# A 2x2 block scheme with seven products for the feed-forward of a hybrid trunk layer

## The chip, the cores and the metric

The kernel runs on one core of a Trainium2 chip. The core has a matrix engine (TensorE, PE in the rows), a vector engine (VectorE, DVE), a scalar engine (ScalarE, ACT), GpSimd (POOL) and SyncE (SP), which here only issues DMA transfers. The metric is the device time of one execution in microseconds (us), the median of several runs.

## The reference

One layer over 1024 tokens of width 1024, in fp32. Three token mixers run on a combined projection of `h` and are concatenated; the rest is an output projection, a residual norm, a gated feed-forward of width 2816 (22 blocks of 128) with a gated per-layer embedding, and a second residual norm:

```
h = layer_norm(x, ln_in_g, ln_in_b)
...
mix = jnp.concatenate([o_a, o_b, o_c], axis=-1) @ w_out[i]
h = layer_norm(DEEPNORM_ALPHA * h + mix, ln1_g[i], ln1_b[i])
gate, up = jnp.split(h @ w_gate_up[i], 2, axis=-1)
ffn = (jax.nn.silu(gate) * up) @ w_down[i]
ple = jax.nn.sigmoid(h @ ple_w_gate[i]) * (p[i] @ ple_w_proj[i])
h = layer_norm(DEEPNORM_ALPHA * h + ffn + ple, ln2_g[i], ln2_b[i])
```

## The kernel before

Every product is made in three matmuls. An operand is split into a high part (a cast to the rounded format on ScalarE) and a low part (the subtraction `sub_lo`, L106, on VectorE, for one weight page in four on GpSimd); high by high, high by low and low by high are added in PSUM. A weight page is 128 x 1024; `wpage` loads and splits it.

The program text is straight-line; a framework schedules it and sets the order of each engine's queue. Each engine, and SP's DMA queue, works its instructions off in that order. Ahead of the change lie the input norm, projections, the three mixers and attention (to about 514.5 us); they stay as they are. Attention stores its output tiles `ta` to DRAM (`mix_d`, L755), 64 rows for each block.

Then follow four stages. The output projection runs twice over the eight token tiles, for either half of the columns (L767 to L789): it loads the mixers' outputs (`mixT`, L772), splits them, and takes 24 matmuls of 512 columns (`op`). In the second pass each tile is normed (`ln_stats`, `ln_apply`) and transposed into `hThi`/`hTlo`. The gate of the embedding (`pgt`, L793 to L805) goes through four quarters of 256 columns. The feed-forward goes through PARTS of three or four blocks f (L808 to L848): gate and up of a block, silu and product (`sil`, `act`), then for all eight tiles the down matmuls of the part (`dn`), added to `r_t` by VectorE (L844). In the last part each tile is normed and stored (`out`, L848).

## Time and profile before

| what | value |
|---|---|
| runs, us | 1439.05, 1440.24, 1440.18; median 1440.18 |
| profiled execution, span | 1436.9 us, 3.3 below the median |
| TensorE busy | 1393.6 us, 97% of the span |
| VectorE busy | 660.0 us, 46% |
| ScalarE busy | 420.3 us, 29% |
| GpSimd busy | 209.2 us, 15% |
| bytes moved by DMA | 133.69 MB, mean 93 GB/s |

Times in rows are from the start of the profiled span. What lies around the span (the 3.3 us) is taken as unchanged. Matmuls overlap in the trace, so the cost of one is the distance between starts, not its own duration.

### The profile page before, as it was taken

How to read it: one execution, taken by the hardware profiler on the slowest of the kernel's cores; microseconds unless marked ns; L12 is line 12 of the kernel's file. 1: busy time of each engine (PE TensorE's matmuls, PEld its weight loads, DVE VectorE, ACT ScalarE, POOL GpSimd, SP SyncE). 2: the span in 40 equal slices, each digit the busy share in tenths (PEclk: the TensorE clock that was granted, in tenths of full speed). 3: DMA queues.
4: the chain of work that ended last, by engine and by line, in shares of the span. 5: the costliest groups of instructions: out<-in, count | busy, mean ns of one | idle time of the engine just before them, and what ended most of it. 6: DMA issues, size and time to landing. Idle time of an engine off the chain costs nothing.

```text
span 1436.9 us, 18294 instructions
## 1 busy us (share of the span) xinstructions
PE 1393.6 (97%) x7264; PEld 1188.4 (83%) x7264; DVE 660.0 (46%) x1019; ACT 420.3 (29%) x791; POOL 209.2 (15%) x225
## 2 busy tenths in 40 slices
PE   6999999999899999999999999999999999999996
PEld 4888998987688878899988888888888888888885
DVE  7832695455778854973322232312332223223248
ACT  5542122452677733431221020120210211202100
POOL 3220111312233301520000000000000000000013
PEclk9999999999899999999999999999999999999999
DMA  8731021445944246232211110210311201202112
GB/s 325 263 101 59 28 67 45 146 169 183 337 111 104 60 137 225 74 122 77 86 44 44 45 59 30 73 45 15 88 44 35 69 30 44 74 16 73 30 44 103
DMA packets 55717, 133.69 MB, mean 93 GB/s; under 512 B 6736, under 2 KB 22096, under 8 KB 54096
## 3 DMA queue, kind: packets, MB, share of 16 engines
q1 hardware_dynamic: 55632, 132.52, 29.1%
q8 instruction: 57, 0.93, 0.3%
q14 instruction: 28, 0.23, 0.0%
HBM read 100.12 MB, written 32.37 MB: 92 GB/s over the span
## 4 chain that ended last, share of the span: by engine, by line
PE 67%; DVE 2%; ACT 2%; issue 1%; POOL 1%; DMA 1%; POOLq 0%; ACTq 0%; SPq 0%; DVEq 0%
PE gate L357 6%; PE dn L843 6%; PE gate L356 6%; PE gate L359 6%; PE up L359 6%; PE up L356 6%; PE up L357 6%; PE dn L840 6%; PE dn L839 6%; PE pgt L240 2%; PE pgt L241 2%; PE pgt L242 2%; PE pt L735 2%; PE op L783 1%; PE sc L715 1%
## 5 line engine op out<-in xcount | busy, mean ns | idle before, releaser
L117 ACT CAST whi<-raw 128x1024 fp32r<-128x1024 f32 (+3 forms) x101 | 104.7, 1037 | 607.0 <-PE dn L840 219.6
L106 DVE TENSOR_TENSOR wlo<-raw,whi 128x1024 fp32r<-128x1024 f32 (+3 forms) x77 | 99.5, 1294 | 177.4 <-ACT whi L117 136.0
L106 POOL TENSOR_TENSOR wlo<-raw,whi 128x1024 fp32r<-128x1024 f32 (+1 forms) x24 | 57.3, 2386 | 784.9 <-ACT whi L117 784.9
L844 DVE TENSOR_TENSOR r<-r,dn 128x1024 f32<-128x1024 f32 x56 | 68.0, 1220 | 161.7 <-PE dn L843 161.3
L357 PE MATMUL gate<-hTlo,whi 128*128 128x512 f32 x352 | 137.0, 389 | 0.0
L356 PE MATMUL gate<-hThi,whi 128*128 128x512 f32 x352 | 136.9, 389 | 0.0
L356 PE MATMUL up<-hThi,whi 128*128 128x512 f32 x352 | 136.9, 389 | 0.0
L357 PE MATMUL up<-hTlo,whi 128*128 128x512 f32 x352 | 136.9, 389 | 0.0
L840 PE MATMUL dn<-wlo,act 128*128 128x512 f32 x352 | 136.9, 389 | 0.0
L839 PE MATMUL dn<-whi,act 128*128 128x512 f32 x352 | 136.8, 389 | 0.0
L822 DVE TENSOR_TENSOR sil<-up,sil 128x512 f32<-128x512 f32 x44 | 28.3, 685 | 199.3 <-PE up L359 199.3
L359 PE MATMUL up<-hThi,wlo 128*128 128x512 f32 x352 | 108.7, 389 | 0.0
L359 PE MATMUL gate<-hThi,wlo 128*128 128x512 f32 x352 | 108.4, 389 | 0.0
L843 PE MATMUL dn<-whi,act 128*128 128x512 f32 x352 | 107.7, 389 | 0.0
L840 PEld LDWEIGHTS dn<-wlo,act 128*128 128x128 f32 x352 | 66.1, 188 | 13.8
L357 PEld LDWEIGHTS up<-hTlo,whi 128*128 128x128 f32 x352 | 66.1, 188 | 13.7
L359 PEld LDWEIGHTS up<-hThi,wlo 128*128 128x128 f32 x352 | 66.0, 188 | 13.7
L356 PEld LDWEIGHTS up<-hThi,whi 128*128 128x128 f32 x352 | 66.1, 188 | 13.7
L839 PEld LDWEIGHTS dn<-whi,act 128*128 128x128 f32 x352 | 66.1, 188 | 13.7
L357 PEld LDWEIGHTS gate<-hTlo,whi 128*128 128x128 f32 x352 | 66.1, 188 | 13.7
L843 PEld LDWEIGHTS dn<-whi,act 128*128 128x128 f32 x352 | 66.1, 188 | 13.7
L356 PEld LDWEIGHTS gate<-hThi,whi 128*128 128x128 f32 x352 | 66.1, 188 | 13.7
(275 smaller groups left out, 2982.3 us busy)
## 6 DMA issues: line engine op xcount, KB each, us to landing
raw<-in_w_gu_dram SPq DMA_DIRECT2D x44, 512.0 KB, 3.5
raw<-in_w_dn_dram SPq DMA_DIRECT2D x22, 512.0 KB, 3.9
mixT<-mix_d SPq DMA_DIRECT2D x16, 512.0 KB, 3.5
x<-in_x_dram SPq DMA_DIRECT2D x8, 512.0 KB, 6.6
h_d<-x SPq DMA_DIRECT2D x8, 512.0 KB, 5.0
pl_d<-plo SPq DMA_DIRECT2D x16, 256.0 KB, 4.6
hx<-h_d SPq DMA_DIRECT2D x16, 256.0 KB, 3.4
raw<-in_w_out_dram SPq DMA_DIRECT2D x8, 512.0 KB, 7.6
```

The source lines that it names most:

```text
L106: eng.tensor_tensor(out=lo, in0=src, in1=hi, op=ALU.subtract)
L117: nc.scalar.copy(out=hi[:, :w], in_=raw[:, :w])
L240: mm(ps, th, wh, start=(k == 0), stop=False)
L241: mm(ps, th, wl, start=False, stop=False)
L242: mm(ps, tl, wh, start=False, stop=(k == NK - 1))
L356: mm(pss[hf], wh, hThi[hf][:, k, :], start=(k == 0), stop=False)
L357: mm(pss[hf], wh, hTlo[hf][:, k, :], start=False, stop=False)
L359: mm(pss[hf], wl, hThi[hf][:, k, :], start=False, stop=(k == NK - 1))
L839: mm(ps[:, c], ah, wd[k][0][:, c], start=(k == 0), stop=False)
L840: mm(ps[:, c], ah, wd[k][1][:, c], start=False, stop=False)
L843: mm(ps[:, c], al, wd[k][0][:, c], start=False, stop=(k == nf - 1))
L844: V.tensor_tensor(out=r_t[t], in0=r_t[t], in1=ps, op=ALU.add)
```

## The change

*Pools.* The pools of the stages up to attention close before the output projection; later stages have pools of their own on the same bytes, whose tiles wait only for users of earlier tiles on these bytes.

*Output projection.* One pass over the eight tiles, both halves of the columns in turn, so `mixT` is loaded and split once. All eight pages of `w_out` are held. The normed rows `h1` and the transposed `hT` are also stored to DRAM.

*Gate of the embedding.* Two halves of 512 columns instead of four quarters; the sum of residual and embedding goes to DRAM (`r_d`).

*Gate and up.* For each block f the product of weights (gate and up rows by two halves of the 1024 inputs) and `hT` (two halves of inputs by two halves of tokens) is made of 7 products instead of 8, each of 4 x 3 matmuls of 512 columns. The sums of weight blocks (`block_sums`, 4 for each f) and of the blocks of `hT` are made on GpSimd; seven operand pairs for each f are split by ScalarE and VectorE. The result `x` goes to DRAM (`x_d`), and for each pair of blocks, j, `down_operands` makes four sums on GpSimd, splits them and stores them (`a_d`).

*Down.* Eleven pairs j in CHUNKS of one or two; in a chunk each tile pair (i, i+4) has 7 products with the operands reloaded (`a_load`, `x_load`, the latter split again). Of the twelve products of a chunk that ScalarE copies out of PSUM, GpSimd adds the copy to `r_t`; the other sixteen VectorE adds from PSUM. The last chunk norms and stores each row in halves.

```diff
-PARTS = ((0, 3), (3, 6), (6, 9), (9, 12), (12, 15), (15, 18), (18, 22))
...
-        mp = ctx.enter_context(tc.tile_pool(name="mp", bufs=1))
-        pp = ctx.enter_context(tc.tile_pool(name="pp", bufs=1, space=bass.MemoryType.PSUM))
+        wpool = ctx.enter_context(tc.tile_pool(name="wpool", bufs=1))
+        front = ExitStack()
+        mp = front.enter_context(tc.tile_pool(name="mp", bufs=1, reuse_waits="tile"))
+        pp = front.enter_context(tc.tile_pool(name="pp", bufs=1, space=bass.MemoryType.PSUM, reuse_waits="tile"))
...
+        def split(hi, lo, src):
+            nc.scalar.copy(out=hi, in_=src)
+            sub_lo(V, lo, src, hi)
...
+        def mix_load(t):
+            mx = op.tile([P, 2, NK, P], F32R, tag="mix", name=nm("mixT"), bufs=3)
+            mr = mx[:, 1].bitcast(F32)
+            dma(out=mr, in_=mix_d[t // 4][t % 4])
+            nc.scalar.copy(out=mx[:, 0], in_=mr)
+            sub_lo(V, mx[:, 1], mr, mx[:, 0])
+            return mx
...
+        wo = []
+        waiting = None
+        for t in range(NT):
+            hx = op.tile([P, D], F32, tag="hx", name=nm("hx"), bufs=2)
+            mx = mix_load(t)
+            dma(out=hx, in_=h_d[t])
+            if t == 0:
...
+            h1 = op.tile([P, D], F32, tag="h1", name=nm("h1"), bufs=2)
+            for hf in range(2):
+                cs = slice(hf * 512, hf * 512 + 512)
+                if t == 0:
+                    for u in range(4):
+                        wo.append(wpage(A["w_out"][hf * 4 + u]) if hf == 0 else
+                                  wpage(A["w_out"][hf * 4 + u], spot=(None if u == 0 else op)))
+                ps = ps_("Z", "op")
                 for k in range(NK):
...
-                V.scalar_tensor_tensor(out=r_t[t][:, cs], in0=hx, scalar=ALPHA, in1=ps, op0=ALU.mult, op1=ALU.add)
...
+                V.scalar_tensor_tensor(out=h1[:, cs], in0=hx[:, cs], scalar=ALPHA, in1=ps, op0=ALU.mult, op1=ALU.add)
+                if hf == 0 and waiting is not None:
+                    h_transposed(*waiting)
+            mv = ln_stats(h1, D, "l")
+            ln_apply(h1, h1, mv, ln1[:, 0, :], ln1[:, 1, :], G if t < 6 else V)
+            waiting = (t, h1)
+        h_transposed(*waiting)
+        op_ctx.close()
...
+        for hf in range(2):
+            wq = [wpage(A["w_pg"][hf * 4 + u]) for u in range(4)]
+            cs = slice(hf * 512, hf * 512 + 512)
+            for t in ((0, 1, 2, 3, 4, 5, 6, 7), (4, 5, 6, 7, 0, 1, 2, 3))[hf]:
+                pl = t2("cp", 3, "pl")
                 dma(out=pl, in_=pl_d[t][:, cs])
...
+                dma(out=hx, in_=h1_d[t][:, cs])
+                ps = ps_("Z", "pgt")
+                c = slice((t % 4) * P, (t % 4 + 1) * P)
+                for k in range(NK):
...
-            for f in range(f0, f1):
-                wg = wpage(A["w_gu"][f])
-                pgu = psu("gate")
-                T_mm([pgu[:, 0:512], pgu[:, 512:1024]], wg)
-                wu = wpage(A["w_gu"][NF + f])
-                pup = [psb("up"), psb("up")]
-                T_mm(pup, wu)
...
+        HOP = {1: HB[0, 0], 2: HB[1, 0], 3: HB[1, 1], 4: TB[4], 5: TB[1], 6: TB[2], 7: TB[3]}
...
+        def wpair(src, pool=None, tag="W", bufs=10):
+            w = (pool or wpool).tile([P, 2, 512], F32R, tag=tag, name=nm("wp"), bufs=bufs)
+            split(w[:, 0, :], w[:, 1, :], src)
+            return w
...
+            if sign > 0:
+                G.tensor_tensor(out=s1, in0=a21, in1=a22, op=ALU.add)
+                G.tensor_tensor(out=s2, in0=s1, in1=a11, op=ALU.subtract)
+                G.tensor_tensor(out=s3, in0=a11, in1=a21, op=ALU.subtract)
+                G.tensor_tensor(out=s4, in0=a12, in1=s2, op=ALU.subtract)
+                return {1: a11, 2: a12, 7: s3, 6: s2, 4: a22, 5: s1, 3: s4}
...
+        ORDER = (1, 2, 7, 6, 4, 5, 3)
+        BANK = {1: "Y", 6: "Y", 5: "Y", 3: "Y", 2: "Z", 7: "W", 4: "W"}
+        OPENS = (1, 2, 7)
...
+                g, u = pages
+                ops = block_sums(g[:, :512], g[:, 512:], u[:, :512], u[:, 512:], 1, s2k)
+                self.w = {m: wpair(ops[m]) for m in ORDER}
...
+            def product(self, m):
...
+                w, b = self.w[m], HOP[m]
+                for k in range(4):
...
+                    mm(o, w[:, 0, ks], b.at(0, k), start=(m in OPENS and k == 0), stop=False, skip_group_check=True)
+                    mm(o, w[:, 0, ks], b.at(1, k), start=False, stop=False, skip_group_check=True)
+                    mm(o, w[:, 1, ks], b.at(0, k), start=False, stop=(k == 3), skip_group_check=True)
+                x = self.x
+                if m in (1, 7, 6):
+                    c = t2("cp", 3)
+                    nc.scalar.copy(out=c, in_=o)
+                    setattr(self, f"c{m}", c)
+                elif m == 2:
+                    self.g0 = t2("g", 2)
+                    V.tensor_tensor(out=self.g0, in0=o, in1=self.c1, op=ALU.add)
+                    act(out=self.g0, in_=self.g0, func=AF.Silu)
+                elif m == 4:
+                    V.tensor_tensor(out=x[:, :512], in0=o, in1=self.c6, op=ALU.add)
+                    V.tensor_tensor(out=x[:, :512], in0=x[:, :512], in1=self.g0, op=ALU.mult)
+                elif m == 5:
+                    V.tensor_tensor(out=x[:, 512:], in0=o, in1=self.c7, op=ALU.add)
+                elif m == 3:
+                    g1 = t2("g", 2)
+                    act(out=g1, in_=o, func=AF.Silu)
+                    V.tensor_tensor(out=x[:, 512:], in0=x[:, 512:], in1=g1, op=ALU.mult)
+        def down_operands(j, x0, x1):
+            a11, a21, a12, a22 = x0[:, :512], x0[:, 512:], x1[:, :512], x1[:, 512:]
+            s = {}
+            def step(m, in0, in1, how):
+                def run():
+                    a, b = (s[q] if isinstance(q, int) else q for q in (in0, in1))
+                    s[m] = t2("q", 2, "s")
+                    G.tensor_tensor(out=s[m], in0=a, in1=b, op=how)
+                    st = gu.tile([P, 2, 2, 256], F32R, tag="st", name=nm("st"), bufs=2)
+                    sv = s[m].rearrange("p (q n) -> p q n", q=2)
+                    split(st[:, :, 0, :], st[:, :, 1, :], sv)
+                    dma(out=a_d[j][m].rearrange("q p a n -> p q a n"), in_=st.bitcast(F32))
+                return run
+            return [step(5, a21, a22, ALU.add), step(6, 5, a11, ALU.subtract),
+                    step(3, a12, 6, ALU.subtract), step(7, a11, a21, ALU.subtract)]
+        CHUNKS = [(0,), (1, 2), (3, 4), (5, 6), (7, 8), (9, 10)]
...
+        def a_load(js):
+            at = [{}, {}]
+            for p in range(2):
+                for m in (7, 6, 5, 3):
+                    at[p][m] = hb_tile([P, len(js), 2, 256], "A")
+                    for u, j in enumerate(js):
+                        dma(out=at[p][m][:, u].bitcast(F32), in_=a_d[j][m][p])
+            return at
...
+        def finish(g):
+            g.product(3)
+            dma(out=x_d[g.f], in_=g.x)
+            done.append(g.x)
+            if g.f % 2:
+                steps.extend(down_operands(g.f // 2, done[-2], done[-1]))
+        for f in range(NF):
+            g = Group(f)
+            g.product(1)
+            if prev is not None:
+                finish(prev)
+            for m in ORDER[1:-1]:
+                g.product(m)
+                if steps:
+                    steps.pop(0)()
+            prev = g
+        first = a_load(CHUNKS[0])
+        finish(prev)
+        for step in steps:
+            step()
...
+                r0, r1 = r_t[self.i], r_t[self.i + 4]
+                r = {1: r0[:, :512], 2: r0[:, :512], 7: r1[:, 512:], 6: r1[:, :512], 4: r1[:, :512],
+                     5: r1[:, 512:], 3: r0[:, 512:]}[m]
+                if m in (1, 7, 6):
+                    c = d2("cp", 6)
+                    nc.scalar.copy(out=c, in_=o)
+                    G.tensor_tensor(out=r, in0=r, in1=c, op=ALU.add)
+                else:
+                    V.tensor_tensor(out=r, in0=r, in1=o, op=ALU.add)
...
+        def norm_out(t):
+            mv = ln_stats(r_t[t], D, "l")
+            for hf in range(2):
+                cs = slice(hf * 512, hf * 512 + 512)
+                ln_apply(r_t[t][:, cs], r_t[t][:, cs], mv, ln2[0][:, cs], ln2[1][:, cs])
+                dma(out=out[t][:, cs], in_=r_t[t][:, cs])
+        def close_pair(pair, last):
+            for d in pair:
+                d.product(3)
+                if last:
+                    norm_out(d.i)
+        def x_load(js, at):
+            for p in range(2):
+                for m, f, s0 in ((1, 0, 0), (2, 1, 0), (4, 1, 512)):
+                    xs = dn.tile([P, len(js), 256], F32, tag="xs", name=nm("xs"), bufs=3)
+                    for u, j in enumerate(js):
+                        dma(out=xs[:, u], in_=x_d[2 * j + f][:, s0 + p * 256:s0 + (p + 1) * 256])
+                    at[p][m] = hb_tile([P, len(js), 2, 256], "A")
+                    split(at[p][m][:, :, 0, :], at[p][m][:, :, 1, :], xs)
+        ln2 = None
+        for ci, js in enumerate(CHUNKS):
+            last = ci == len(CHUNKS) - 1
+            at, bt = first if ci == 0 else a_load(js), []
+            x_load(js, at)
+            for j in js:
+                raws = []
+                for f in (2 * j, 2 * j + 1):
+                    raw = wpool.tile([P, 1024], F32, tag="raw", name=nm("raw"), bufs=3)
+                    dma(out=raw, in_=A["w_dn"][f])
+                    raws.append(raw)
+                w0, w1 = raws
+                ops = block_sums(w0[:, :512], w0[:, 512:], w1[:, :512], w1[:, 512:], -1, s2k)
+                b = {}
+                for m in ORDER:
+                    nw[0] += 1
+                    b[m] = wpair(ops[m]) if nw[0] % 17 < 10 else wpair(ops[m], dn, "WC", 7)
+                bt.append(b)
...
+            for pair in ([(0, 1), (2,), (3,)] if last else [(0, 1), (2, 3)]):
...
+                for d in pair:
+                    d.product(1)
+                if pending:
+                    close_pair(*pending.pop())
+                for m in ORDER[1:-1]:
+                    for d in pair:
+                        d.product(m)
+                        if last and m == 5:
+                            norm_out(d.i + 4)
+                pending.append((pair, last))
+        close_pair(*pending.pop())
+        dn_ctx.close()
```

On SP's queue, at the end of attention and the start of the output projection (`ta`: an attention tile that is stored, `mixT`: a mixer tile that is loaded), before:

```order
L755 DMA mix_d_33_100<-ta_983_5016 64x4x128
L772 DMA mixT_1038_5203<-mix_d_33_100 128x1024
L772 DMA mixT_1041_5235<-mix_d_33_100 128x1024
L772 DMA mixT_1044_5267<-mix_d_33_100 128x1024
L772 DMA mixT_1047_5299<-mix_d_33_100 128x1024
L755 DMA mix_d_34_101<-ta_1017_5167 64x4x128
L772 DMA mixT_1050_5331<-mix_d_34_101 128x1024
```

and with the change:

```order
L757 DMA mix_d_33_103<-ta_983_5019 64x4x128
L757 DMA mix_d_34_104<-ta_1017_5170 64x4x128
L809 DMA mixT_1125_5296<-mix_d_33_103 128x1024
L832 DMA hx_1124_5295<-h_d_1_71 128x1024
L834 DMA ln1t_5278<-in_ln1_dram 128x1024
L835 DMA ln1t_5278<-in_ln1_dram 128x1024
L809 DMA mixT_1156_5416<-mix_d_33_103 128x1024
```

Four loads of `mixT` stood ahead of the last store of `ta`; now that store stands ahead of the first load.

On SP's queue, where the feed-forward goes from gate/up to down (`raw`: a weight page), before, at the last such place but one:

```order
L112 DMA raw_1487_9437<-in_w_gu_dram 128x1024
L112 DMA raw_1495_9504<-in_w_dn_dram 128x1024
L112 DMA raw_1498_9510<-in_w_dn_dram 128x1024
L112 DMA raw_1501_9516<-in_w_dn_dram 128x1024
L112 DMA raw_1512_9682<-in_w_gu_dram 128x1024
```

and with the change at the only one (`st`: a split sum of the last pair; `xs`: a part of `x` that chunk 0 loads and splits; `r`: a row of the residual):

```order
L1134 DMA raw_2023_10421<-in_w_dn_dram 128x1024
L1037 DMA x_d_1063_5221<-x_1906_9939 128x1024
L1013 DMA a_d_1105_5263<-st_1925_10077 128x2x512
L1013 DMA a_d_1106_5264<-st_1927_10083 128x2x512
L1013 DMA a_d_1104_5262<-st_1929_10089 128x2x512
L1013 DMA a_d_1107_5265<-st_1931_10095 128x2x512
L1121 DMA xs_1932_10107<-x_d_1042_5200 128x256
L1121 DMA xs_1934_10112<-x_d_1043_5201 128x256
L1121 DMA xs_1936_10117<-x_d_1043_5201 128x256
L1076 DMA r_1957_10170<-r_d_1034_5192 128x1024
```

Before, only weight pages are loaded there, and operands stay in SBUF; now five stores of the last pair stand ahead of the first loads of chunk 0, which come from other blocks.

On GpSimd's queue in the feed-forward, before (the low part of every fourth weight page, and the norm's scalars at the end):

```order
L106 TENSOR_TENSOR wlo_1595_10528<-raw_1593_10525,whi_1594_10527 128x1024
L106 TENSOR_TENSOR wlo_1618_10723<-raw_1616_10720,whi_1617_10722 128x1024
L135 TENSOR_SCALAR til_1628_10770<-til_1628_10770 128x1
L136 TENSOR_TENSOR til_1628_10770<-til_1628_10770,mhalf_66 128x1
L135 TENSOR_SCALAR til_1631_10806<-til_1631_10806 128x1
```

and with the change in a middle chunk of down (`s1` to `s4`: sums of weight blocks for the next chunk; `r`: a residual row, `cp`: a product that ScalarE has copied out of PSUM):

```order
L946 TENSOR_TENSOR s1_2151_11100<-raw_2149_11096 128x512
L1097 TENSOR_TENSOR r_1957_10170<-r_1957_10170,cp_2106_10811 128x512
L947 TENSOR_TENSOR s2_2152_11101<-raw_2150_11098,s1_2151_11100 128x512
L1097 TENSOR_TENSOR r_1959_10174<-r_1959_10174,cp_2108_10821 128x512
L1097 TENSOR_TENSOR r_1958_10172<-r_1958_10172,cp_2112_10861 128x512
L948 TENSOR_TENSOR s3_2153_11102<-raw_2150_11098,raw_2149_11096 128x512
L1097 TENSOR_TENSOR r_1960_10176<-r_1960_10176,cp_2114_10871 128x512
L1097 TENSOR_TENSOR r_1958_10172<-r_1958_10172,cp_2115_10880 128x512
L1097 TENSOR_TENSOR r_1960_10176<-r_1960_10176,cp_2116_10889 128x512
L949 TENSOR_TENSOR s4_2154_11103<-raw_2150_11098,s2_2152_11101 128x512
```

A chunk of two j has twenty of these, eight sums and twelve residual adds, in one queue.

## Rows read from the trace of the kernel before

**Rows 1.** The page: busy us, share and instructions of each engine
```profile
PE 1393.6 (97%) x7264; PEld 1188.4 (83%) x7264; DVE 660.0 (46%) x1019; ACT 420.3 (29%) x791; POOL 209.2 (15%) x225
```

**Rows 2.** The page: the chain that ended last, by engine
```profile
PE 67%; DVE 2%; ACT 2%; issue 1%; POOL 1%; DMA 1%; POOLq 0%; ACTq 0%; SPq 0%; DVEq 0%
```

**Rows 3.** Windows of two stretches without stalls, columns as named in its first line
```profile
core 0: us, PE busy (x) PEld busy (x) DVE busy (x) ACT busy (x) POOL busy (x), PEclk, DMA share, GB/s
720.00:1370.00 650.00, 650.00 (x2869) 538.21 (x2868) 175.26 (x177) 107.43 (x144) 36.08 (x15) 1.00 0.15 47
628.00:660.00 32.00, 32.00 (x269) 32.00 (x269) 13.13 (x27) 6.54 (x14) 0.00 (x0) 1.00 0.26 79
```

**Rows 4.** Groups by form: xcount | busy us, mean ns | idle before
```profile
L357 PE MATMUL gate<-hTlo,whi 128*128 128x512 f32 x352 | 137.0, 389 | 0.0
L240 PE MATMUL pgt<-whi,hThi 128*128 128x256 f32 x256 | 73.5, 287 | 3.3 <-DVE r L784 3.3
```

**Rows 5.** Windows after the output projection, same columns
```profile
612.00:614.00 2.00, 0.00 (x0) 0.00 (x0) 2.00 (x3) 0.03 (x1) 2.00 (x2) 1.00 0.87 332
616.00:618.00 2.00, 2.00 (x12) 2.00 (x11) 2.00 (x3) 1.98 (x3) 0.75 (x1) 0.50 0.60 227
616.00:628.00 12.00, 12.00 (x95) 11.99 (x94) 11.08 (x15) 6.60 (x10) 3.97 (x3) 0.90 0.32 113
```

**Rows 6.** Chain that ended last, 604 to 618: start, us, what
```profile
615.25 0.58 PE pgt L240
```

**Rows 7.** Chain that ended last, 505 to 517
```profile
509.79 3.57 DMA mixT<-mix_d
...
513.43 1.05 ACT mixT L773
```

**Rows 8.** Timeline of PE, 513 to 517: start, us, what [idle before]
```profile
514.53 0.50 PE L781 MATMUL op<-whi,mixT 128*128 128x512 f32 x1 [0.86 <-ACT mixT L773]
```

**Rows 9.** Timeline of SP's queue, 500 to 530
```profile
516.35 0.58 SPq L755 DMA_DIRECT2D mix_d<-ta  x1
```

**Rows 10.** Tile rhl: ns min/median/max, first and last start, forms
```profile
L106 POOL TENSOR_TENSOR rhl<-ra,rhl x6: 1288/1298/1301, 335.4 to 353.4; 128x512 fp32r<-128x512 f32 x4, 32x512 fp32r<-32x512 f32 x2
```

**Rows 11.** Timeline of DVE, 576 to 592
```profile
577.49 1.21 DVE L106 TENSOR_TENSOR mixT<-mixT 128x1024 fp32r<-128x1024 f32 x1
...
581.92 2.05 DVE L106 TENSOR_TENSOR mixT<-mixT 128x1024 fp32r<-128x1024 f32 x1
```

**Rows 12.** Timeline of POOL, 575 to 592
```profile
580.51 2.38 POOL L155 TENSOR_TENSOR r<-r,ln 128x1024 f32<-128x1024 f32 x1 [2.96 <-DVE r L154]
582.98 1.05 POOL L135 TENSOR_SCALAR til<-til 128x1 f32<-128x1 f32 x1
```

**Rows 13.** Timeline of DVE, 920 to 930 (up comes from PSUM)
```profile
925.43 1.29 DVE L822 TENSOR_TENSOR sil<-up,sil 128x512 f32<-128x512 f32 x2 [11.13 <-PE up L359]
```

**Rows 14.** Timeline of POOL, 920 to 930
```profile
924.78 2.41 POOL L106 TENSOR_TENSOR wlo<-raw,whi 128x1024 fp32r<-128x1024 f32 x1 [50.45 <-ACT whi L117]
```

**Rows 15.** Lines 821 and 823 of ACT: ns min/median/max, first and last start
```profile
L821 ACT ACTIVATE sil<-gate x44: 587/592/600, 720.8 to 1372.7; 128x512 f32<-128x512 f32 x44
...
L823 ACT CAST act<-sil x44: 619/622/627, 730.3 to 1383.7; 128x512 fp32r<-128x512 f32 x44
```

**Rows 16.** DMA issues: KB each, median us from issue to landing
```profile
pl<-pl_d SPq DMA_DIRECT2D x32, 128.0 KB, 2.3
...
out_dram<-r SPq DMA_DIRECT2D x8, 512.0 KB, 2.6
...
mix_d<-ta SPq DMA_DIRECT2D x16, 128.0 KB, 2.6
```

**Rows 17.** Windows of a stretch with much DMA, columns as in rows 3
```profile
20.00:24.00 4.00, 4.00 (x14) 3.52 (x15) 3.58 (x5) 2.21 (x3) 0.00 (x0) 1.00 1.02 402
```

**Rows 18.** Timeline of PE, 1425 to the end
```profile
1425.42 0.61 PE L843 MATMUL dn<-whi,act 128*128 128x512 f32 x2
```

**Rows 19.** Timeline of DVE, 1424 to the end
```profile
1428.40 1.28 DVE L143 BATCH_NORM_STATS2 bnst<-r 128x6 f32<-128x512 f32 x2
...
1431.96 1.29 DVE L158 SCALAR_TENSOR_TENSOR r<-r,til,ln 128x1024 f32<-128x1024 f32 x1 [0.72 <-POOL til L136]
```

241 lines of the change are left out of this document (164 added, 77 removed).

## The prediction

> **What bounds the kernel now.** I read the page first: the busy line gives TensorE 1393.6 of 1436.9 us, while VectorE, ScalarE and GpSimd have 660, 420 and 209 [rows 1], and the chain that ended last is PE for 67% with no other engine above 2% [rows 2]. A table by windows then says what a matmul costs where nothing else interferes. In 720:1370, all feed-forward, PE is busy for all of 650 us at a granted clock of 1.00 and starts 2869 matmuls, so a 512-column matmul occupies 226.6 ns; in 628:660, where only the 256-column gate projection runs, it is 32.00/269 = 119.0 ns [rows 3]. The groups show the counts: each of the nine feed-forward lines has 352 matmuls, 3168 in all, and the gate projection has three lines of 256 [rows 4]. (The 389 ns there are pipelined, from issue to end; the pitch is what a matmul costs.) So the feed-forward is 3168 x 0.2266 = 717.9 us, half the span, without a stall. A matmul removed there is worth its whole 0.2266 us, unless what replaces it makes PE wait. The other engines have room on average, but the change gives nearly all new work to them, so they are to be counted stage by stage.
>
> **What it removes.** Gate/up goes from 22 x 96 = 2112 matmuls to 22 x 7 x 12 = 1848, and down from 1056 to 11 x 84 = 924. Tile shape and one weight load per matmul stay, so -396 x 0.2266 = **-89.7 us**. A gate projection of 768 x 0.119 = 91.4 becomes 384 x 0.2266 = 87.0, **-4.4**. The output projection keeps 384 matmuls.
>
> **The hole after the output projection.** In 612:614 PE runs nothing [rows 5]; the chain shows its next matmul at 615.25, so some 3.3 us are lost [rows 6]. In 616:618 the granted clock is 0.50, the 1.2 GHz level: over 616:628 the mean 0.90 means 1.2 us lost, and half of 615.25 to 616 another 0.4, together 1.6 [rows 5]. The last tile's norm sits there alone. With the change the first half of the gate projection takes the tiles in their order, tile 7 last: seven tiles of 24 x 0.2266 = 5.4 us lie over the norm of tile 7. I take **-5.0**; bounds 0 (the hole moves) and -6.
>
> **The start of the output projection, by SP's order.** Now the first mix load is issued at 509.79, lands after 3.57 us, is cast in 1.05, and PE starts at 514.53 [rows 7, 8]. The last store of the attention output is issued at 516.35 and takes 0.58 on SP's queue [rows 9]; before, four mix loads stood in front of it. Now they stand behind it: 516.9 + 3.6 + 1.05 = 521.5, 7.0 us later, and the clock, which fell in the 3.3 us hole, is taken to fall here too, another 1.6: **+8.6**. Below: 0, if the attention's tail gets faster by as much; above: 10, with the wider w_out staging.
>
> **Gate/up, steady.** Two f take 168 x 0.2266 = 38.1 us of PE. GpSimd does 12 sums; a 128x512 one takes 1.30 us [rows 10]. VectorE does 22 operations with two SBUF inputs and 6 with one from PSUM; 512 columns take 0.645 (two in 1.29 with a PSUM input [rows 13]; 1.21 for 1024 columns from SBUF [rows 11] is no more). The trace shows that the first kind and a GpSimd operation exclude each other: the 1.21 us subtraction takes 2.05 when it starts at 581.92, while GpSimd runs from 580.51 to 582.89 [rows 11, 12], whereas two with a PSUM input keep 0.645 each inside the GpSimd operation of 924.78 [rows 13, 14]. GpSimd's next operation started 0.09 after the last [rows 12], so a sum costs 1.38. Together the exclusive part is 12 x 1.38 + 22 x 0.645 = 30.8 of 38.1 us. It fits: **0**; if that cover went, the excess over 38.1 would be added for each of eleven pairs.
>
> **From gate/up to down.** SP's order puts the last pair's x store and four a_d stores ahead of chunk 0's x loads, which need none of them, and ScalarE's order does the same. PE has only the last product 3 (12 matmuls) and six of product 7 after that. From the last gate/up matmul the chain is: silu 0.6 [rows 15], multiply 0.65, a GpSimd sum 1.3, cast 0.62 [rows 15], subtraction 0.65 to 1.3, store 2.6 (for 512 KB to the output as for 128 KB [rows 16]), two further casts and subtractions that wait for a free staging buffer, about 2; then the x load with 1 KB rows, 2.3 [rows 16], cast 0.4. That is 11.1 to 11.8, and 0.6 of the issue for each of five stores on SP [rows 9] adds 3, half of it hidden: 13 us after the last gate/up matmul. The six matmuls of product 7 hide 1.4 of them, the clock adds 1.6: about **+14** with rounding up for waits in a row. Bounds: 8 (stores overlap wholly) and 20.
>
> **Chunk 0** has one j, so 84 matmuls, 19.0 us, but it carries a full round of residual adds (12 on GpSimd) and the first five sums of chunk 1: 17 x 1.38 = 23.5. The excess of 4.5 and the a_d loads of chunk 1, which wait for the buffers of the gate/up operands, make **+7**; bounds 0 and 15.
>
> **Down, steady (four chunks of two j, 38.1 us of PE each).** GpSimd has 12 residual adds and 8 sums, 20 x 1.38 = 27.6 us. VectorE has 36: 16 adds from PSUM and 20 splits with two SBUF inputs, 12.9 us. The exclusive part is 27.6 + 12.9 = 40.5 us, 2.4 more than PE needs, and the order in each queue adds waits. I take 4 per chunk, **+16**. If nothing collides it is 0, as each engine alone has under 28 us; if all 36 VectorE operations are held, 27.6 + 23.2 = 50.8, +12.7 per chunk or +51. Rows with a PSUM input speak for the lower third [rows 13]. Transfers: 16 a_d loads of 256 KB, 12 x loads of 128 KB and four pages of 512 KB are 7.9 MB in 38 us, 207 GB/s; 402 GB/s were reached in 20:24 [rows 17]. Hidden.
>
> **The tail.** Now the last two matmuls end at 1426.0, and the span 10.9 us later [rows 18]: an add, two statistics in 1.28, the norm's two passes, the last 1.29, and a store of 2.6 [rows 16, 19]. In the change the last chunk holds eight norms: on VectorE 16 statistics, 32 normalising halves and 13 adds, 61 x 0.645 = 39.3 us, with 8 short aggregations about 41, and with waits for GpSimd's part of each norm some 46 (chosen). They can start when the first rows close, about 25 us before PE ends. So 46 - 25 = 21, store 3, about 25 in place of 10.9: **+14**, bounds 4 and 20.
>
> **Sum.** 1436.9 - 89.7 - 4.4 - 5.0 + 8.6 + 14 + 7 + 16 + 14 = 1397.4 us of span. The median of the runs, 1440.2, is 3.3 above the profiled span: about **1400** as timed.
>
> **A rule on the clock.** The stretch after the hole, 616:628, has a mean granted clock of 0.90 [rows 5], and my sum pays that once at each of two stops. The Trainium skill, page "TensorE: Matmul & The Clock Gate", section "HAM oscillation — how this bites in real kernels", tells of a kernel in which each wait for a transfer lets the clock fall, so that the price is paid at every step and not once. By the row paid twice the sum is 1400; by that rule, paid in each chunk of down, it would be the third rival's time below.
>
> **Rivals.**
> 1. *The waits are hidden.* The queues interleave well: boundary 8, chunk 0 and steady down 0, tail 8, start 8.6. 1436.9 - 99.1 + 24.6 + 3.3 = 1366. For it: no engine alone is over 28 of 38 us. Against it: the exclusion rows and 40.5 over 38.1. Chance 0.19.
> 2. *GpSimd and VectorE serialise in down (slower side).* Every residual add waits its turn and PE waits for PSUM banks. Without the steady term the time is 1384.7; over four chunks, the time before is reached when a chunk lasts 38.1 + 55.5/4 = 52 us. Full serialisation of 50.8 comes just short; with a wait for GpSimd's order in each add it passes: 54 us a chunk gives 1448. For it: GpSimd's doubled residual add on the same rows; against it: the PSUM-input row. Chance 0.07.
> 3. *The clock falls in every chunk.* If all of down, 924 x 0.2266 = 209 us, ran at the mean 0.90 of rows 5, 209 x 0.1/0.9 = 23 us more: 1423. For it: several waits a chunk; against it: they are short, and the clock stayed 1.00 through all short gaps. Chance 0.06.
> That the matmuls are not cut can't be: they are counted.
>
> **Numbers.** My forecast is 1400, own range 1378 to 1422, chance 0.66; rival 1 has 0.19, rival 2 0.07, rival 3 0.06, and 0.02 is left for something just below 1440. Low 1362 takes in rival 1, high 1425 rival 3. About 0.2%, 1437.3 to 1443.1, is what a measurement of this kernel can tell from no change. Faster: 0.66 + 0.19 + 0.06 = 0.91; the same 0.03; slower 0.06.
>
> **What would show it.** 1848 and 924 feed-forward matmuls at 226.6 ns; the first output-projection matmul near 521 and 0.50 of the clock behind it; a hole of about 12 us between gate/up and down that ends with a split of an x load; chunks of about 42 us with VectorE subtractions stretched beside GpSimd; about 25 us after the last matmul. It would be wrong if gate/up itself stalls (then some sum is late), if PE has no hole at the boundary, or if a chunk lasts 38 or 52 us.

## The result, and the profile after

The changed kernel takes 1405.11 us (median of 4 runs, 1403.80 to 1406.67), the kernel before 1439.62 on the same chip: a ratio of 0.976, interval 0.9749 to 0.9776, 34.5 us less. The forecast was 1400 with a range of 1362 to 1425. The profiled execution has a span of 1404.1 us; its own time was 1405.89.

The page of the changed kernel: the busy line.

```profile
PE 1311.1 (93%) x6484; PEld 1097.1 (78%) x6484; DVE 938.0 (67%) x1375; ACT 587.9 (42%) x1170; POOL 560.6 (40%) x472
```

TensorE lost 82.5 us of busy time against [rows 1], and outside it the span has 93.0 us where it had 43.3: the products are saved, and 50 us of idle time came instead. VectorE is busy 278 us longer and GpSimd 351; a part of that is time in which one holds up the other, as the account of the steady part of down shows. TensorE's longest waits after the attention of the changed kernel say where the idle time stands (waiting line and what it waited for: us in total, times, longest).

```profile
PE dY L1088 <- ACT A L770: 13.2, 1, 13.2
PE dY L1088 <- DVE r L1099: 8.9, 5, 2.8
PE op L848 <- ACT mixT L810: 8.6, 1, 8.6
PE pgt L911 <- ACT sg L915: 4.4, 1, 4.4
PE dW L1088 <- DVE r L1099: 4.2, 2, 2.9
PE pgt L912 <- DVE wlo L107: 2.7, 2, 1.5
```

The same by windows (stretch, length; busy us and count of PE, PEld, DVE, ACT, POOL; granted clock, DMA share, GB/s):

```profile
515.00:525.00 10.00, 2.85 (x7) 2.27 (x8) 5.32 (x3) 3.02 (x4) 2.34 (x1) 0.52 0.81 290
626.00:636.00 10.00, 5.63 (x25) 4.47 (x24) 3.76 (x7) 4.70 (x8) 0.00 (x0) 0.77 0.62 210
720.00:1130.00 410.00, 410.00 (x1811) 339.49 (x1810) 261.87 (x304) 168.84 (x302) 198.31 (x129) 1.00 0.40 140
1150.00:1160.00 10.00, 8.62 (x28) 6.36 (x28) 8.07 (x9) 7.89 (x18) 6.04 (x5) 0.81 0.98 345
1150.00:1215.00 65.00, 54.67 (x209) 41.85 (x210) 51.82 (x60) 29.92 (x59) 47.45 (x33) 0.89 0.83 287
1215.00:1325.00 110.00, 109.70 (x485) 90.50 (x484) 88.58 (x101) 51.95 (x93) 83.04 (x57) 1.00 0.63 205
1325.00:1384.80 59.80, 53.47 (x228) 42.69 (x226) 50.19 (x69) 14.08 (x26) 33.24 (x29) 0.98 0.19 65
```

Against [rows 3], the steady stretch of gate/up has not changed: 410.00/1811 = 226.4 ns a matmul, clock 1.00, although VectorE, ScalarE and GpSimd now have 262, 169 and 198 us of work in it. The stop that [rows 5, 6] show at 612 to 615 stands again at 626 to 636. Two stops are new or longer (515 to 525, 1136 to 1150), chunk 0 and the start of chunk 1 run at 0.89, and 1215 to 1325, the middle of down, is full.

The chain of the changed kernel from the last gate/up matmul (start, us, what) shows the longest stop.

```profile
1135.56 0.61 ACT g L997
1136.19 0.70 DVE x L998
...
1136.96 1.27 POOL s L1009
...
1138.30 1.27 POOL s L1009
1139.60 0.63 ACT st L770
1140.25 0.70 DVE st L107
1140.97 3.34 DMA a_d<-st
1144.39 0.63 ACT st L770
1145.04 0.70 DVE st L107
...
1147.58 4.64 DMA xs<-x_d
1152.24 0.40 ACT A L770
```

Silu, multiply, two sums in a row on GpSimd, a split, a store, a split again, issues on SP's queue and the load of x: the steps are those of the forecast. The x loads that TensorE needs at 1150 stand in this queue; the chain shown goes on to a later one.

The stop inside the gate projection is to be read on ScalarE (timeline of the changed kernel: start, us, line, operation, tile; in brackets the idle time ahead and what ended it).

```profile
629.22 1.01 ACT L821 COPY hTr<-hT 128x1024 f32<-128x1024 f32 x1 [4.80 <-PE hT L818]
630.26 1.32 ACT L770 CAST B<-hTr 128x256 fp32r<-128x256 f32 x4
631.60 1.28 ACT L915 ACT_TABLE_LOAD   x1
632.90 1.09 ACT L915 ACTIVATE sg<-pgt 128x512 f32<-128x512 f32 x2
```

The sigmoids of gate tiles 0 and 1 stand in ScalarE's queue behind the copy of tile 7's transposes, which waits for tile 7's norm. Two PSUM banks hold gate tiles, both are full until those sigmoids, and TensorE stops after tile 1.

Last, the end of the changed kernel: TensorE's last row.

```profile
1384.20 0.63 PE L1090 MATMUL dY<-wp,A 128*128 128x512 f32 x1
```

From the end of the last matmul to the end of the span it is 1404.1 - 1384.8 = 19.3 us, before 10.9 [rows 18].

### The profile page after: what moved, and what is told of

Same layout as the page of the kernel before. It is cut to its first block, busy times and chain, and to the rows that moved or that the text cites. A ratio compares the mean times of both kernels' runs of the same rounds, so it can differ in the third digit from the quotient of the medians.

```text
span 1404.1 us, 18592 instructions
## 1 busy us (share of the span) xinstructions
PE 1311.1 (93%) x6484; PEld 1097.1 (78%) x6484; DVE 938.0 (67%) x1375; ACT 587.9 (42%) x1170; POOL 560.6 (40%) x472
## 4 chain that ended last, share of the span: by engine, by line
PE 84%; DVE 5%; DMA 5%; ACT 2%; issue 2%; POOL 1%; SPq 0%; POOLq 0%; DVEq 0%; ACTq 0%
PE Y L978 6%; PE Y L980 6%; PE Y L979 6%; PE W L979 3%; PE W L980 3%; PE W L978 3%; PE dY L1088 2%; PE dY L1089 2%; PE dY L1090 2%; PE op L848 2%; PE op L849 2%; PE op L850 2%; PE pt L737 2%; PE lv L427 2%; DMA rb<-hT_d 1%
## 5 line engine op out<-in xcount | busy, mean ns | idle before, releaser
L107 DVE TENSOR_TENSOR wp<-s,wp 128x512 fp32r<-128x512 f32 x132 | 130.6, 1001 | 47.6 <-ACT wp L770 47.4
L1097 POOL TENSOR_TENSOR r<-r,cp 128x512 f32<-128x512 f32 x72 | 107.5, 1511 | 29.0 <-ACT cp L1096 28.4
L107 DVE TENSOR_TENSOR wp<-raw,wp 128x512 fp32r<-128x512 f32 x99 | 101.9, 1035 | 16.1 <-ACT wp L770 16.1
L770 ACT CAST wp<-s 128x512 fp32r<-128x512 f32 x132 | 80.3, 622 | 48.8 <-PE dY L1090 13.6
L770 ACT CAST wp<-raw 128x512 fp32r<-128x512 f32 x99 | 60.7, 621 | 93.1 <-PE W L980 38.3
L1088 PE MATMUL dY<-wp,A 128*128 128x512 f32 x176 | 69.9, 401 | 23.2 <-ACT A L770 13.2
L1089 PE MATMUL dY<-wp,A 128*128 128x512 f32 x176 | 69.8, 397 | 0.3 <-DVE wp L107 0.3
L1090 PE MATMUL dY<-wp,A 128*128 128x512 f32 x176 | 68.3, 394 | 1.7 <-DVE A L107 1.7
L978 PE MATMUL Y<-B,wp 128*128 128x512 f32 x176 | 68.6, 390 | 0.8 <-DVE x L994 0.8
L980 PE MATMUL Y<-B,wp 128*128 128x512 f32 x176 | 68.5, 389 | 0.0
L978 PE MATMUL W<-T,wp 128*128 128x512 f32 x176 | 68.5, 389 | 0.0
L979 PE MATMUL W<-T,wp 128*128 128x512 f32 x176 | 68.5, 389 | 0.0
L980 PE MATMUL W<-T,wp 128*128 128x512 f32 x176 | 68.5, 389 | 0.0
L978 PE MATMUL Y<-T,wp 128*128 128x512 f32 x176 | 68.5, 389 | 0.0
L979 PE MATMUL Y<-T,wp 128*128 128x512 f32 x176 | 68.5, 389 | 0.0
L979 PE MATMUL Y<-B,wp 128*128 128x512 f32 x176 | 68.5, 389 | 0.0
L980 PE MATMUL Y<-T,wp 128*128 128x512 f32 x176 | 68.5, 389 | 0.0
L107 DVE TENSOR_TENSOR st<-s,st 128x512 fp32r<-128x512 f32 x44 | 54.1, 1232 | 13.2 <-ACT st L770 11.4
```

The lines of the kernel that those rows point to most:

```text
L107: eng.tensor_tensor(out=lo, in0=src, in1=hi, op=ALU.subtract)
L770: nc.scalar.copy(out=hi, in_=src)
L978: mm(o, w[:, 0, ks], b.at(0, k), start=(m in OPENS and k == 0), stop=False, skip_group_check=True)
L979: mm(o, w[:, 0, ks], b.at(1, k), start=False, stop=False, skip_group_check=True)
L980: mm(o, w[:, 1, ks], b.at(0, k), start=False, stop=(k == 3), skip_group_check=True)
L1088: mm(o, a[:, k, 0, cs], b[:, 0, :], start=(m in OPENS and k == 0), stop=False, skip_group_check=True)
```

## The experiments

Each ratio below is to the kernel before on the same chip (medians 1438.6 to 1439.4). The first eight experiments are compared with the changed kernel's 1405.1 unless another is named. The four runs of one kernel lie 1.4 to 5.7 us apart, so differences of 3 or 4 us are barely clear of that.

**The boundary: x ahead of the last pair's stores.** Edit: chunk 0's x operands are loaded and split in place before the last gate/up pair is finished.

```
         first = a_load(CHUNKS[0])
+        for p in range(2):
+            for m, f, s0 in ((1, 0, 0), (2, 1, 0), (4, 1, 512)):
+                a = hb_tile([P, 1, 2, 256], "A")
+                xr = a[:, :, 1, :].bitcast(F32)
+                dma(out=xr[:, 0], in_=x_d[f][:, s0 + p * 256:s0 + (p + 1) * 256])
+                split(a[:, :, 0, :], a[:, :, 1, :], xr)
+                first[p][m] = a
         finish(prev)
...
-            x_load(js, at)
+            if ci:
+                x_load(js, at)
```

> Chunk 0's loads of x stand ahead of the last pair's stores, and are split in place, so they need no staging tile; nothing else is changed. Theory: the 13.2 us hole between gate/up and down, and the half clock behind it (about 1.9 us), come from the order of the queues alone. Then down begins at once, the hole is under 2 us, and the median falls by 13 to 15 us, from 1405 to about 1391. Rival: VectorE, ScalarE and GpSimd use the hole to get ahead (sums and splits for chunk 0 and 1); without it they are late, the waits in chunk 0 (7 to 10 us now) grow by most of what was gained, and the median is 1399 or more.

Measured 1405.0, ratio 0.9765 (0.9746 to 0.9784): no change. The rival's number, but not by the rival's mechanism. TensorE's stop is now a wait of 10.9 us for `cp`, ScalarE's copies of chunk 0's first products out of PSUM, and ScalarE's rows in this kernel show why they are late:

```profile
1150.51 0.62 ACT L770 CAST st<-s 128x512 fp32r<-128x512 f32 x1 [6.72 <-DMA a_d<-st]
1153.05 0.62 ACT L770 CAST st<-s 128x512 fp32r<-128x512 f32 x1 [1.93 <-DMA a_d<-st]
1153.57 1.07 ACT L1103 COPY cp<-dY 128x512 f32<-128x512 f32 x2
```

The casts of the last pair's block sums wait for a staging buffer, which a store holds, and the copies stand behind them. The hole moved from the x load to ScalarE's queue. The waits for `r`, which the rival saw growing, are as before (13.5 us, in the changed kernel 13.7).

**The boundary, second try.** The same edit, and the last pair's sums and staging take other buffers (the staging in the weight pool) and stand behind chunk 0's first products in the program:

```
-                    s[m] = t2("q", 2, "s")
+                    s[m] = s2k("s") if late[0] else t2("q", 2, "s")
...
         finish(prev)
-        for step in steps:
-            step()
+        late[0] = True
...
                 pending.append((pair, last))
+                while steps:
+                    steps.pop(0)()
```

> As the first experiment, and the last pair's four sums come behind chunk 0's first tile pair in the program, with staging tiles from the weight pool, so that no cast waits for a store. Theory (the hole moved into ScalarE's queue, where the copies of down's first products stood behind casts that waited for a_d stores): the wait for copies in chunk 0, 13.0 us there, shrinks to 4 to 6, and the median is 1396 to 1399. Rival (GpSimd's four sums and VectorE are the limit whatever the order; the time is given back in chunk 0): the sum of waits between 1135 and 1190 stays at 23 us or more, and the median is 1403 or more.

1401.6, ratio 0.9734 (0.9719 to 0.9748): 3.5 us less, between the theories. TensorE waits 9.1 us for `cp` instead of 13.2 for the x load. Of these, 2.7 come from ScalarE: the order that the scheduler made still has three of the four casts ahead of the copies. The other 6.4 come from GpSimd: a copy there waits for one of the six `cp` buffers, which the residual adds free, and the first of these adds starts only at 1154.51, behind nine block sums in GpSimd's queue. All waits in 1135 to 1190 are 12.0 us, where the rival had 23 or more.

**The start: mix tile 0 ahead of the attention's last stores.** Edit (core): tile 0 of mix goes into two weight pages and is loaded before the attention's pools close; w_out's other pages move to the freed pool.

```
+        w0 = [wpool.tile([P, 1024], F32R, tag="W", name=nm("mix0"), bufs=10) for _ in range(2)]
+        m0r = w0[1].bitcast(F32)
+        dma(out=m0r.rearrange("p (k n) -> p k n", k=NK), in_=mix_d[0][0])
+        nc.scalar.copy(out=w0[0], in_=m0r)
+        sub_lo(V, w0[1], m0r, w0[0])
         front.close()
...
-                                  wpage(A["w_out"][hf * 4 + u], spot=(None if u == 0 else op)))
+                                  wpage(A["w_out"][hf * 4 + u], spot=op))
```

> The first tile of mixer outputs is loaded into the weight pool, so it doesn't wait for the pools of attention and stands ahead of attention's last store in SP's queue; two more pages of w_out move to the stage's own pool in exchange. Theory: the 8.7 us hole at the start of the output projection comes from that order. Then its first matmul starts at about 514.5 and not 522.15, the half clock behind it goes too, and the median falls by 8 to 10 us, to about 1396. Rival: transfers crowd there (DMA share 0.81 in 515:525); the next pages and tiles come late, the wait moves to the second half or the second tile, and the gain is under 3 us.

1409.3, ratio 0.979 (0.9775 to 0.9806): 4 us more. The first out-projection matmul came at 517.13 instead of 522.15, as meant, but TensorE then waited 3.6 us for pages of w_out and 3.2 for the next mix tile, and the start was given back by the gate projection: its stop ends at 638.20, in the changed kernel at 633.55. Its parts (the pages that moved, the transfers at a DMA share of 0.98 in 525 to 535) weren't told apart.

**Down: no residual adds on GpSimd.** VectorE adds all products straight from PSUM; GpSimd keeps its sums.

```
-                if m in (1, 7, 6):
+                if m == 0:
```

> In down, VectorE adds all 28 products of a chunk from PSUM; ScalarE copies none and GpSimd makes only the 8 sums. Theory (GpSimd and VectorE exclude each other): the waits in chunk 0, about 10 us and 5 us of half clock, come from GpSimd's adds holding up VectorE's splits; they shrink by 8 us or more, middle chunks stay without waits (exclusive part 8 x 1.38 + 20 x 0.645 = 24 us, VectorE in all 48 x 0.66 = 32 of 38), and the median is about 1396. Rival (VectorE's own queue is the limit): products 1 and 6 wait in PSUM for an engine with twelve more operations, PE waits longer for banks, and the median is 1405 or more.

1397.1, ratio 0.9706 (0.9691 to 0.972): -8.0, the number of the theory of held splits. VectorE gets more operations and yet is in time sooner: TensorE's waits for `r` in down fall from 13.7 us to 4.0; 4.0 us of waits for ScalarE's casts in chunk 0 come new. The windows row of this kernel over the middle of down:

```profile
1200.00:1340.00 140.00, 140.00 (x619) 115.93 (x618) 119.47 (x179) 44.44 (x75) 38.95 (x28) 1.00 0.59 192
```

VectorE is at 85% here and TensorE never waits. But the gain did not come from there: the middle was already full in the changed kernel. From the first down matmul behind the stop to the end of the last it is 222.5 us instead of 234.8; the tail gives 2.2 back. Only a part of this is where the theory put it: the waits in chunk 0 fall by 3.8 us (10.1 to 6.3, not by 8) and the half clock there by 2.6, and the waits in the last chunk, which the theory did not name, by 4.5. The edit also takes twelve copies a chunk from ScalarE, so it does not show by itself how much is GpSimd's hold on VectorE.

**Down: more on GpSimd.** One add more per round goes to GpSimd, 24 operations a chunk.

```
-                if m in (1, 7, 6):
+                if m in (1, 7, 6) or (m == 5 and n == 2 and ln2 is None):
```

> In the four middle chunks of down one more product of each tile pair, the fifth, is copied by ScalarE and added by GpSimd instead of VectorE: GpSimd has 24 operations a chunk and not 20. Theory (the count of exclusive time holds, and the forecast 4 us a chunk only didn't show because the lead of about 5 us was enough): exclusive part 24 x 1.38 + 20 x 0.645 = 46 us against 38.1 of PE, 8 us more in each of four chunks, less the lead, 1425 to 1437. Rival (much of it overlaps after all; each engine only has to fit by itself): 24 x 1.5 = 36 of 38.1 us fits, and the median stays within 4 us of 1405.

1408.8, ratio 0.9779 (0.976 to 0.9799): +3.7, the rival's "within 4", and hardly outside the spread. The window over the middle of down of this kernel:

```profile
1216.00:1326.00 110.00, 105.49 (x462) 86.03 (x461) 86.72 (x87) 51.48 (x93) 95.79 (x64) 1.00 0.63 209
```

TensorE is idle 4.5 of these 110 us, where the changed kernel has 0.3, and it waits mainly for splits (`wp`, 3.7). GpSimd is at 87% and VectorE at 79%, so neither is full by itself: that speaks against the rival's mechanism, and for time that the two hold in common. The cover was there, and it is used up at 24 operations.

**The gate projection: six PSUM banks for gate tiles instead of two.** Each of the three tags stands for two banks.

```
-                ps = ps_("Z", "pgt")
+                bk = "ZYW"[t % 3]
+                ps = ps_(bk, "pgt")
```

> The gate of the embedding takes its PSUM tiles from three tags in turn, six banks and not two. Theory (the hole behind the output projection moved: the sigmoid of the first tiles stands behind the transposes of tile 7 on ScalarE, and PE stops when both banks are full): the 4.4 us wait and the half clock behind it go, and the median falls by 4 to 6 us, to about 1400. Rival (PE then meets the next thing that is late, the sums of hT blocks and the second half's pages, with 2.7 us of waits now): the waits in this stage stay above 5 us, and the median falls by less than 2.

1395.3, ratio 0.969 (0.9676 to 0.9704): -9.8, more than the 4 to 6 expected. A row of this kernel by windows:

```profile
626.00:636.00 10.00, 10.00 (x50) 8.37 (x49) 3.27 (x8) 2.21 (x6) 0.00 (x0) 1.00 0.23 94
```

The 4.4 us stop is gone, and so is the half clock behind it. Gone too are the 2.7 us of waits for `wlo`, which in the changed kernel stand at 671 to 675, where the pages of the second half of the columns come; the theory had left these out, and why they went was not tested. From the first out-projection matmul to the first of down behind the boundary it is 619.5 us instead of 627.9: 8.4 less, 7.1 of waits and 1.3 net of clock.

**Three together:** the adds on VectorE, the six banks, and the last norms' sums on ScalarE.

```
-            mv = ln_stats(r_t[t], D, "l")
+            mv = ti("l")
+            for c, func in ((4, AF.Copy), (5, AF.Square)):
+                junk = d2("cp", 6, "junk").bitcast(BF16)
+                act(out=junk, in_=r_t[t], func=func, accum_out=mv[:, c:c + 1])
```

> All residual adds of down on VectorE from PSUM, six banks for the gate of the embedding, and the statistics of the second norm on ScalarE (two passes that sum x and its square) in place of VectorE. Theory: adds 8, banks 4 to 5, and the tail: VectorE has eight times 1.28 us of statistics less, so the 20 us behind the last matmul become about 13; together 19, about 1386. Rival for the tail: each norm's chain gets longer by ScalarE's second pass, and VectorE's passes stay in one queue; the tail stays above 18 us, and the median is about 1392.

1383.8, ratio 0.9611 (0.9595 to 0.9627). 1405.1 - 8.0 - 9.8 = 1387.3, so 3.5 are left for the statistics if the three add up. The tail is 15.1 us.

**Four together:** that, and the second try at the boundary.

> The third kernel of this set and the first one together. Theory (the hole between gate/up and down is worth its own 6 us beside the others): about 1379. Rival (with the adds on VectorE, which also splits the last pair's sums, the two crowd into the same 30 us and most of it is given back): within 2 us of the third kernel.

1375.2, ratio 0.9553 (0.9538 to 0.9567), the best version: 64.2 us less than before and 30 less than the change. With the adds off ScalarE's copies and GpSimd the boundary edit is worth 8.6, where alone it was worth 3.5: the wait for GpSimd's adds that was left there has gone. What remains of the stop (TensorE's timeline, VectorE's, and a line of the chain of this kernel):

```profile
1147.74 0.79 PE L1097 MATMUL dY<-wp,A 128*128 128x512 f32 x1 [14.19 <-DVE r L1108]
```

```profile
1143.06 1.75 DVE L107 TENSOR_TENSOR wp<-raw,wp 128x512 fp32r<-128x512 f32 x1
1144.95 2.14 DVE L107 TENSOR_TENSOR wp<-s,wp 128x512 fp32r<-128x512 f32 x2
1147.01 0.67 DVE L1108 TENSOR_TENSOR r<-r,dY 128x512 f32<-128x512 f32 x1
```

```profile
1139.14 6.34 DMA r<-r_d
```

TensorE waits for the first residual add. The loads of the rows of r are issued from 1137.73 on, behind the loads of chunk 1, and at a DMA share of 1.02 in 1140 to 1160 they take 6 to 11 us. But the add did not wait for its row: the first two rows landed at 1144.22 and 1145.48, and the third only after the add had begun. VectorE goes straight from weight splits into the add; it stands behind them in VectorE's queue, and the last of them are splits of sums that GpSimd makes.

**That kernel with r's rows on another queue.**

```
+        for t in (0, 4, 1, 5, 2, 6, 3, 7):
+            r_t[t] = dn.tile([P, D], F32, tag="r", name=nm("r"), bufs=NT)
+            nc.scalar.dma_start(out=r_t[t], in_=r_d[t])
```

> The four-part kernel, with the eight loads of residual rows for down issued on ScalarE's DMA queue, ahead of the first chunk in the program. What is left of the hole between gate/up and down there is 14.2 us of waiting for the first residual add, which starts at 1147.0, 9.3 us after the row's load was issued behind eleven loads for chunk 1. Theory (the order of SP's queue sets it): the rows come 2 to 6 us earlier, and the median falls from 1375 to 1370 to 1373. Rival (the transfers themselves are the limit, DMA share 1.02 in 1140:1160): the rows land as late as before among the others, and the median stays within 1.5 us.

1383.8, ratio 0.9604 (0.9579 to 0.9629): 8.6 more than 1375.2, and both theories missed. The rows landed about as late as before, as the rival had it (the first at 1142.95, the last at 1157.29; before 1144.22 and 1156.29). ScalarE's rows of this kernel, first the loads of r by themselves (ns min/median/max of one issue):

```profile
L1112 ACTq DMA_DIRECT2D r<-r_d x8: 326/327/511, 1136.4 to 1150.9; - x8
1136.43 14.75 ACTq L1112 DMA_DIRECT2D r<-r_d  x8
1151.28 0.62 ACT L770 CAST st<-s 128x512 fp32r<-128x512 f32 x1 [15.42 <-DMA r<-r_d]
```

Eight issues held ScalarE's queue for 14.75 us at a DMA share of 1.02 in 1136 to 1151. One issue takes about a third of a microsecond; the rest of the time the queue waited between them, and what ended the longer waits was the landing of an earlier transfer: the last issue begins at 1150.85, 0.02 us after the fourth of these rows landed. The cast of a staging tile stood behind the issues, VectorE's split behind the cast, and the first residual add behind the split, at 1152.53; TensorE's stop grew to 19.56.

**That kernel without the statistics on ScalarE**, to price them alone (the edit of the three, undone).

> The four-part kernel without the statistics on ScalarE (VectorE makes them as in the changed kernel). Theory (VectorE's backlog behind the last matmul sets the tail): about 21 us behind the last matmul and not 15, median 1381 to 1383. Rival (the two passes on ScalarE lengthen each norm as much as they relieve VectorE): within 2 us of 1375.

1382.5, ratio 0.9597 (0.9567 to 0.9627): +7.3, as the theory had it. The last matmul ends 3.1 us later, since the statistics stand among the last adds on VectorE's queue again (TensorE's waits for `r` behind chunk 0 are 4.8 us instead of 1.8), and the tail is 19.0 instead of 15.1.

**That kernel with fewer loads ahead of the out-projection:** tile 0's row of h is loaded behind its first half, the norm's vectors on ScalarE's queue.

```
-            dma(out=hx, in_=h_d[t])
-            if t == 0:
-                dma(out=ln1[:, 0, :], in_=A["ln1"][0:1, :].partition_broadcast(P))
-                dma(out=ln1[:, 1, :], in_=A["ln1"][1:2, :].partition_broadcast(P))
+            if t:
+                dma(out=hx, in_=h_d[t])
```

> The four-part kernel; at the start of the output projection the first residual row is loaded behind the first tile of mixer outputs and its matmuls in the program, and the norm's gain and bias come on ScalarE's queue. Theory (the first tile's load lands in 5.34 us beside three others, 3.57 us in the kernel before): 1.5 to 2 us off the 7 us hole, median 1373 to 1374. Rival (the next tile and the pages of w_out take the place of what is moved): no change within 1 us.

1375.1, ratio 0.954 (0.952 to 0.9561): no change. The mix tile's load took 5.56 us although the others no longer stand right behind it; in the four-part kernel's own profile it took 3.8, so the 5.34 from which the theory started was that of one execution. The loads behind the mix tile are not what makes it late.

## Why the prediction held, and which step did not

The time fell on the forecast's side and 5 us above it. By its own steps:

- **Feed-forward, -89.7.** Right: groups of 176, 88 or 44 where [rows 4] has 352, at 226.4 ns a matmul, with no stall in 720 to 1130. The cover named for the sums was there.
- **Start of the out-projection, +8.6.** Right in its mechanism, and lucky in its parts: the first matmul at 522.15 (forecast 521.5), 7.6 later than in [rows 8], and 1.7 of half clock. The chain of the changed kernel has the forecast's steps:

```profile
514.88 0.57 SPq L757
515.63 5.34 DMA mixT<-mix_d
521.06 1.05 ACT mixT L810
```

  The store is issued 1.5 us earlier than in [rows 9], and the load behind it takes 5.34 us instead of the 3.57 of [rows 7]; the two cancel. In the profiles of the nine experiments that leave this place alone the load took 3.7 to 4.4 us, and the first matmul came at 520.8 to 522.4.
- **The hole after the out-projection, -5.0.** Wrong in sign. It moved, which was the forecast's bound of 0, and it is longer: by the experiment with six banks 8.4 us (5.7 without the 2.7 of waits for pages) against the 3.3 + 1.6 worked out of [rows 5, 6], so +3.5. The step that failed is "seven tiles lie over the norm of tile 7": TensorE had the operands, but not the PSUM banks, because the sigmoid that frees a bank stands on ScalarE behind the norm's result. Six banks instead of two removed it.
- **Boundary, +14.** Right: 13.2 us of wait and 1.9 of half clock (10 us at 0.81 from 1150), 15.1.
- **Chunk 0, +7.** Mis-sized: 10.1 us of waits from 1155 to 1184, most of them for `r`, and 5.2 of clock: 15.3, just over its upper bound of 15. The forecast set GpSimd's 17 operations against TensorE's 19.0 us and left out VectorE's splits, which it adds to them in its next step. In the changed kernel both queues are nearly full there:

```profile
1153.00:1184.00 31.00, 20.75 (x76) 14.02 (x75) 30.82 (x34) 15.52 (x31) 29.02 (x19) 0.89 0.96 351
```

  VectorE is busy for 30.82 of 31 us, 21.86 of them in 18 splits, and its adds, for which TensorE waits, stand among these. From 1150.08 to 1384.83 it is 234.8 us for 918 x 0.2266 = 208.0 (six of the 924 matmuls lie ahead of the stop); waits in chunk 0 and 1 of 10.1, clock of 65 x 0.11 = 7.1 with the boundary's 1.9 in it, waits of the last chunk 6.3 and its clock 1.2, and 0.3 between, make 25.0 of these 26.8.
- **Down, steady, +16.** The step that failed most: the exclusive part, priced at 1.38 + 0.645 = 2.03 us a pair. The middle costs 0.3: 110 us hold 485 matmuls, so a chunk lasts 38.1 us, which the prediction itself had named as a sign of being wrong. The timelines of the changed kernel, VectorE first and then GpSimd, where both have work in a row:

```profile
1252.54 1.78 DVE L107 TENSOR_TENSOR A<-xs,A 128x512 fp32r<-128x512 f32 x1
1254.24 1.78 DVE L107 TENSOR_TENSOR wp<-raw,wp 128x512 fp32r<-128x512 f32 x1
1255.94 1.78 DVE L107 TENSOR_TENSOR A<-xs,A 128x512 fp32r<-128x512 f32 x1
1257.65 1.77 DVE L107 TENSOR_TENSOR wp<-s,wp 128x512 fp32r<-128x512 f32 x1
1259.34 0.67 DVE L1099 TENSOR_TENSOR r<-r,dW 128x512 f32<-128x512 f32 x1
```

```profile
1253.73 1.73 POOL L948 TENSOR_TENSOR s<-raw,raw 128x512 f32<-128x512 f32 x1
1255.43 3.44 POOL L1097 TENSOR_TENSOR r<-r,cp 128x512 f32<-128x512 f32 x2
1259.50 1.29 POOL L949 TENSOR_TENSOR s<-raw,s 128x512 f32<-128x512 f32 x1 [0.63 <-DVE wp L107]
```

  They alternate, one of each in 1.70 us, where each alone is 0.60 to 0.67 and 1.29. Twenty such pairs are 34.0 us of 38.1, not 40.5: the stage fits, and the waits of the queues' order, which the forecast added, did not reach TensorE. Not all meet either: of the 57 GpSimd operations in 1215 to 1325, 28 took 1.57 to 1.84 us and 29 took 1.28 to 1.32. The experiment with 24 operations on GpSimd shows the edge: 20 x 1.70 + 4 x 1.30 = 39.2 would be 1.1 over for each chunk; measured are 4.5 us of idle time in 110, 1.6 for 38.1.

  The Trainium skill, page "SBUF — State Buffer", section "Who interferes with whom", says that a VectorE instruction with two SBUF inputs contends with a GpSimd instruction that reads SBUF, and calls the contention an exclusive lock. The alternation agrees; the pair is 0.2 us shorter than 0.60 + 1.29, so not all of an operation is exclusive.
- **Tail, +14.** About right in sum, 15.9, by other parts: 19.3 - 10.9 = 8.4 behind the last matmul, and 7.5 of waits and clock in the last chunk ahead of it. The norms take VectorE's queue from the adds that free PSUM banks, so a part of the tail shows as TensorE's waits. That is shown by the statistics: off VectorE, 3.1 us come from ahead of the last matmul and 3.9 from behind.

With the measured terms the sum is 1436.9 - 89.7 - 4.4 + 3.5 + 9.3 + 15.1 + 15.3 + 0.3 + 15.9 = 1402.2; 1.9 of the span of 1404.1 are not assigned. The forecast of the span, 1397.4, is thus 6.7 low; the median is only 5 off, since it lies 1.0 above the profiled span and not the 3.3 that the forecast added. Two errors of 8.5 and 8.3 upward (the hole, chunk 0) stood against one of 15.7 downward (steady down): the nearness of the total owes something to that.

**The rivals.** The first (waits hidden) was right in steady down alone. The second did not come: a middle chunk of 168 matmuls takes 168 x 110/485 = 38.1 us. The third, the clock falling in each chunk, did not come in the middle chunks: 0.50 in 1140 to 1150, 0.89 over 1150 to 1215, 1.00 over 1215 to 1325. The Trainium skill, page "TensorE: Matmul & The Clock Gate", section "HAM oscillation — how this bites in real kernels", has the price paid at every step. In this trace it is not paid at every wait: of the seven waits of 0.6 to 2.9 us from 1155 to 1184, those ahead of 1170 leave the clock at 1.00 in 1160 to 1170, and the later ones, which follow each other closely, go with one fall, to 0.50 in 1180 to 1185.

**What stays open.** The 14 us before the first add of down in the best version: the add stands behind weight splits in VectorE's queue. Loading r through ScalarE's queue cost more than it gave; an order of VectorE's and GpSimd's queues with the adds ahead of the next weights was not run, so what that wait is worth is not shown. Nor was the start of the out-projection shortened: both tries there left the time as it was or worse. Why the mix tile's load takes 3.7 us in one execution and 5.6 in another is open too.

## What to carry to other kernels

When work is cut from a bounding engine, count per stage what the helpers then hold in common, in every stage and not only in the steady one, and price that from a row in which both really alternate; here the sum of their separate prices was too high, 40.5 us where the rows give 34.0. At a stage boundary list, for each engine's queue, what stands ahead of the first instruction that the bounding engine needs: several of the largest losses here were in-order queues (a mix load behind a store, a sigmoid behind a transposed tile's copy, a PSUM copy behind casts that wait for stores, a residual add behind weight splits). Clearing one queue showed the next: at the boundary the x load, then ScalarE's casts, then GpSimd's sums, then VectorE's splits. And when an add is late, compare the landing of its operand with its start before blaming the load. Before giving a DMA issue to a helper engine, see what that issue will itself wait for.
